# The last rows of a decoder layer: one PSUM bank of 512 columns against two of 256 columns with walked matmuls

## The chip, the cores and the metric

The kernel runs on one core of a Trainium2 chip. Its time is device time in microseconds, the median of several executions; a profile shows one of the executions instruction by instruction. The engines are TensorE (PE, with its weight loads as PEld), VectorE (DVE), ScalarE (ACT), GpSimd (POOL) and SyncE (SP), which issues most DMAs.

## What is computed

One decoder layer in fp32 for 256 prompt rows and 64 sample rows, 320 in all, with D = 2048 and D_FF = 5632. Cut to what matters here:

```
h = x + merged @ w_o
hn = rms_norm(h, g_ffn)
h = h + (silu(hn @ w_gate) * (hn @ w_up)) @ w_down
y = rms_norm(h, g_final)      # y * rsqrt(mean(y*y) + 1e-6) * g_final
```

The change lies in the product with w_down and in the final norm of the first 128 rows. That norm needs the squares of all 2048 columns of a row before it can scale any of them.

## The kernel before

**The precision.** Every fp32 matrix is split into a high part (rounded to the matmul's type, fp32r) and a low part (the rest). A product is made of high x high, high x low and low x high, so each weight tile is loaded raw by SP's queue, copied to `whi` by ACT and subtracted to `wlo` by DVE (`split_to`, L128). PE multiplies without a pause.

**The walk.** `turns` (L101) rearranges an access of s parts and j columns so that four columns of part 0 come first, then four of part 1, and so on. A matmul whose moving operand and output are both rearranged this way computes the same numbers in another order of columns. The rows in SBUF are laid out for it: their parts lie a multiple of 64 columns plus 16 apart (`rows_in`, L109; `a_rows`, L964), in the PSUM bank they lie exactly 64 apart (`fives` and `placed`, 5 parts and 8 parts).

**The down product.** `down(half, c0)` (L985) takes 512 output columns of w_down at a time, for 28 and then for 16 of the 44 blocks of D_FF. It makes the product in two forms at once. Four banks `dn` hold it by feature (features on partitions, rows as columns), with matmuls at L1008 (high weights) and L1016 (low weights), both walked. For the first 128 rows the low part of the activations is multiplied the other way round: the activations `a_low(k)` are the stationary operand and 512 columns of the high weights move, so that a bank holds rows on partitions and features as columns. That is the matmul of L1012, one per block k, not walked. For the first 1536 columns its bank is a `dl` from the pool aux2; for the last 512 (E0 = 1536 on) it is `rowacc`, which isn't read out after half 0 but kept.

**The tail.** For the last 512 columns of half 1 the order is written out by hand (from L1145). The weights of all 16 blocks are held in SBUF. The feature form comes first (L1173, L1178), and only for the 192 rows that need it. Then come 32 matmuls into `rowacc` (L1207), for each block one with `a_first(k)`, the high part of the first 128 rows, and one with `a_low(k)`. After the first 8 of them stand `pn` (L1211), the sum of squares over partitions for the other 192 rows, and four transposes (L1213) which add the first 128 rows of h from its feature form to `rowacc`.

Behind that run two strands. The other 192 rows: DVE makes their factor from pn, multiplies in five pieces (L1228), and SP sends each (L1229). The first 128 rows: ACT squares `rowacc` and sums over its columns (`row_squares`, L1084, the instruction at L1086, with a second one that reads the accumulator), DVE sums the earlier partial sums (L1232), ACT and DVE make the factor `rr` (L1235 to L1238), then DVE, ACT and POOL scale the columns of `y0` (L1240, L1241, L1245), DVE scales `rowacc` by rr and by gfb, the broadcast g_final (L1251), and five DMAs send `y0` (L1242).

`after(...)` fixes the order of issue without a wait on the chip.

Of the kernel before, what the change touches and what calls it, by code (L numbers as in the profile page):

```python
# [8 lines left out]
F32 = mybir.dt.float32  # L9
F32R = mybir.dt.float32r  # L10
AF = mybir.ActivationFunctionType
ALU = mybir.AluOpType
AX = mybir.AxisListType
PSUM = bass.MemoryType.PSUM

D = 2048
# [10 lines left out]
P = 128  # L27
KC = D // P
CW = 256
# [8 lines left out]
E0 = D - 512  # L38
# [14 lines left out]
def hybrid_layer(ctx: ExitStack, tc: tile.TileContext, a: dict, o: list):  # L53
    nc = tc.nc
# [11 lines left out]
    aux = [aux_p.enter_context(tc.tile_pool(name="aux", bufs=4, space=PSUM))]  # L66
# [5 lines left out]
    def ps_aux(name):  # L72
        return aux[0].tile([P, 512], F32, tag="aux", name=name)
# [3 lines left out]
    def u(s):  # L77
        uid[0] += 1
        return f"{s}_{uid[0]}"

    def after(*marks):

        es = ExitStack()
        for m in marks:
            es.enter_context(tc.issue_after(m.ins))
        return es
# [14 lines left out]
    def turns(ap):  # L101

        return ap.rearrange("p s (i b) -> p i s b", b=4)

    def fives(ap):

# [51 lines left out]
    last = {}  # L158
# [78 lines left out]
    ident = cst.tile([P, P], F32, name="ident")  # L237
# [37 lines left out]
    hT = xv[:, VW:VX].rearrange("p (k t) -> p k t", k=KC)  # L275
# [560 lines left out]
    for cp in range(4):  # L836
# [8 lines left out]
        for c in range(2):  # L845
# [13 lines left out]
            n = UL - 2  # L859
            nc.scalar.activation(cv[:, :n], ue[:, 0:n], AF.Copy, scale=wcv[:, ch:ch + 1])  # L860
            for jj in (1, 2):
                nc.vector.scalar_tensor_tensor(
                    cv[:, :n], ue[:, jj:jj + n], wcv[:, jj * 8 + ch:jj * 8 + ch + 1], cv[:, :n],
                    op0=ALU.mult, op1=ALU.add,
# [33 lines left out]
    for mp in range(8):  # L898
        c0 = mp * CW
# [51 lines left out]


    aux_p.close()
    aux[0] = ctx.enter_context(tc.tile_pool(name="aux2", bufs=3, space=PSUM))
    row_p = ctx.enter_context(tc.tile_pool(name="row_p", bufs=1, space=PSUM))
    rowacc = row_p.tile([P, 512], F32, name="rowacc")
    fp = ctx.enter_context(tc.tile_pool(name="fp", bufs=1))
    op = ctx.enter_context(tc.tile_pool(name="op", bufs=1))
    FH = (28, 16)
# [25 lines left out]
    def down(half, c0):  # L985

        nf, f0 = FH[half], half * FH[0]
        ps = [ps_acc(u("dn")) for _ in range(4)]
        low = ps_aux(u("dl")) if c0 < E0 else rowacc
        sets = [[k] for k in range(0, nf, 2)]  # L990
        sets[-2:] = [sets[-2] + sets[-1]]
        for i, k0s in enumerate(sets):
            parts = {}
            for k0 in k0s:
                raw = wp.tile([P, 2, 512], F32, tag="wraw", name=u("wraw"), bufs=4)
                nc.sync.dma_start(raw, w_d[c0 // 512, :, f0 + k0:f0 + k0 + 2, :])
                hi, lo = down_parts()
                split_to(hi, lo, raw)
                for j in range(2):
                    parts[k0 + j] = (hi[:, j, :], lo[:, j, :])  # L1000
            end = i == len(sets) - 1
            order = [(k, c) for k in parts for c in range(4)]
            if end or i == 0:
                order.sort(key=lambda kc: kc[1])
            for k, c, m in in_turn(order, 2 if end else 4):
                cs = slice(c * P, (c + 1) * P)
                if m == 0:
                    nc.tensor.matmul(  # L1008
                        turns(placed(ps[c])), parts[k][0][:, cs], turns(a_move(k)), start=k == 0, stop=False
                    )  # L1010
                elif m == 1 and c == (2 if k > k0s[0] + 1 else 0):
                    nc.tensor.matmul(  # L1012
                        low, a_low(k), parts[k][0], start=k == 0, stop=k == nf - 1 and c0 < E0
                    )
                elif m == 2:
                    last["mm"] = nc.tensor.matmul(  # L1016
                        turns(placed(ps[c])[:, :, 0:JT]), parts[k][1][:, cs], turns(a_move(k)[:, :, 0:JT]),
                        start=False, stop=k == nf - 1,
                    )
            if pending and (end or i == 3):  # L1020
                with after(last["lo"], last["hi"], last["mm"]):
                    pending.pop(0)()
        mark["out"] = []
        for c in range(4):
            k = c0 // P + c
            got, (first, rest) = placed(ps[c]), h_parts(k)
            nc.vector.tensor_add(first, first, got[:, :, 0:JR])
            nc.vector.tensor_add(rest, rest, got[:, :, JR:JT])
            mark["out"].append(nc.vector.tensor_add(rest, rest, got[:, :, JT:]))
        if c0 < E0:  # L1030
            ys = ylow[:, c0:c0 + 512].rearrange("p (a c f) -> p c a f", a=4, c=4)
            got = low.rearrange("p (c a f) -> p c a f", a=4, c=4)
            if half == 0:
                nc.scalar.activation(ys, got, AF.Copy)
            else:
                nc.vector.tensor_add(ys, got, ys)

    for half in range(2):
# [38 lines left out]
        if half == 1:  # L1077
            ya = xp.tile([P, 2, D], F32, tag="xh", name="ya")
            y0, gfb = ya[:, 0, :], ya[:, 1, :]
            nc.gpsimd.dma_start(gfb, a["g_final"].partition_broadcast(P))  # L1080
            ssf = op.tile([P, 5], F32, name="ssf")
            yacc = op.tile([P, TR], F32, name="yacc")

            def row_squares(i, src):  # L1084
                jk = op.tile([P, 512], F32, tag="jk", name=u("jk"))
                nc.scalar.activation(  # L1086
                    jk[:, :src.shape[-1]], src, AF.Square, scale=D ** -0.5, accum_out=ssf[:, i:i + 1]
                )

            turned = {}  # L1090

            def rows_turned(c0):

                x = op.tile([P, 512], F32, tag="jk", name=u("jk")).rearrange("p (b m) -> p b m", b=4)
                nc.vector.transpose(
                    x.rearrange("p b (c f) -> p c b f", c=4),
                    hT[:, c0 // P:c0 // P + 4, 0:P].rearrange("p c (b t) -> p c b t", b=4),
                )
                blocks_out([x[32 * b:32 * b + 32] for b in range(4)], x)
                turned[c0] = x.rearrange("p b m -> p (b m)")  # L1100

            def rows_of(c0):

                y = y0[:, c0:c0 + 512]
                nc.gpsimd.tensor_tensor(y, turned.pop(c0), ylow[:, c0:c0 + 512], op=ALU.add)
                row_squares(c0 // 512, y)
                nc.gpsimd.tensor_tensor(y, y, gfb[:, c0:c0 + 512], op=ALU.mult)

            def rest_square(k):
                sq = tmp("td", "sq")[:, :TR] if k else yacc  # L1110
                nc.scalar.activation(sq, hT[:, k, P:T], AF.Square)
                return sq

            def rest_factor(k):
                rest = hT[:, k, P:T]
                last["hi"] = nc.scalar.activation(rest, rest, AF.Copy, scale=g_fin[:, k:k + 1])

            def rest_of(chunks):

                for k in chunks:  # L1120
                    sq = rest_square(k)
                    if k:
                        nc.vector.tensor_add(yacc, yacc, sq)
                    rest_factor(k)

            warm = op.tile([P, 1], F32, name="warm")
            eps = op.tile([P, 1], F32, name="eps")
            nc.vector.memset(eps, EPS)
            nc.vector.memset(ssf[:, 3:4], EPS)
            with after(last["sig"]):  # L1130
                nc.scalar.activation(warm, ones, AF.Abs_reciprocal_sqrt)
# [8 lines left out]


    nf = FH[1]
    es = slice(E0, D)

    held = []  # L1145
    more = xp.tile([P, 5 * KT * CW + 64], F32R, tag="xl", name="more")
# [55 lines left out]
    for c in range(4):  # L1202
        rest_factor(E0 // P + c)

    for k in range(nf):
        for m, x in enumerate((a_first(k), a_low(k))):
            last["mm"] = nc.tensor.matmul(rowacc, x, held[k][0], start=False, stop=k == nf - 1 and m == 1)  # L1207
        if k == 3:
            with after(last["mm"]):
                pn = ps_aux("pn")  # L1210
                nc.tensor.matmul(pn[:, :TR], ones_r.bitcast(F32), yacc, start=True, stop=True)  # L1211
                for c in range(4):
                    last["mm"] = nc.tensor.matmul(  # L1213
                        rowacc[:, c * P:(c + 1) * P], hT[:, E0 // P + c, 0:P], ident, start=False, stop=False,
                        is_transpose=True,
                    )
    rf, v, t = (op.tile([P, TR], F32, name=n) for n in ("rf", "rv", "rt"))
# [7 lines left out]
    for k0, k1 in ((0, 2), (2, 5), (5, 10), (10, 15), (15, KC)):  # L1225
# [2 lines left out]
            ahead = (nc.vector.tensor_mul(yq, hT[:, k0:k1, P:T], rf.unsqueeze(1).to_broadcast([P, k1 - k0, TR])),)  # L1228
        nc.sync.dma_start(y_r[:, k0:k1, :], yq)  # L1229
    s3, v, r = (op.tile([P, 1], F32, name=n) for n in ("s3", "vf", "rr"))  # L1230
    with after(*ahead):
        nc.vector.tensor_reduce(s3, ssf[:, 0:4], axis=AX.X, op=ALU.add)  # L1232
    row_squares(4, rowacc)
    part = ssf[:, 4:5]
    nc.scalar.activation(r, part, AF.Abs_reciprocal_sqrt, bias=s3)  # L1235
    nc.vector.tensor_scalar(v, part, s3, -0.5, op0=ALU.add, op1=ALU.mult)
    nc.vector.scalar_tensor_tensor(v, r, r, v, op0=ALU.mult, op1=ALU.mult)
# [10 lines left out]
    send(768, 1280, nc.scalar)  # L1248
    with after(sent):
        sent = send(256, 768)  # L1250
    nc.vector.scalar_tensor_tensor(y0[:, es], rowacc, r, gfb[:, es], op0=ALU.mult, op1=ALU.mult)  # L1251
    with after(sent):
        sent = send(1280, E0)
    with after(sent):
# [80 lines left out]
```

## Time and profile before

| | us |
|---|---|
| median of 3 runs | 1592.32 (1591.9 to 1592.51) |
| the profiled execution | 1591.96 |
| its span, first to last instruction | 1590.3 |
| PE busy | 1582.1 |
| DVE busy | 889.6 |
| ACT busy | 645.7 |
| POOL busy | 133.1 |

The span is shorter than the execution's time by 1.66 us, which lie around it. A row of the page or of a view names an engine, a line of the kernel, the operation, what it writes and reads (out<-in), and durations. Durations of consecutive matmuls overlap; the chain of waits is the view that shows their pace. "128*128 128x256" is a matmul with 128 x 128 weights and 256 moving columns. The granted TensorE clock was 0.999 of full.

### The profile page before, as it was taken

The numbers are of one execution on the slowest core, as the hardware profiler recorded it, in microseconds if no ns is written. First come the engines' busy times: TensorE is split into PE (matmuls) and PEld (weight loads), VectorE is DVE, ScalarE is ACT, GpSimd is POOL, SyncE is SP. The second block draws the span as 40 slices with busy tenths as digits, with TensorE's granted clock in tenths as the row PEclk, the third lists the DMA queues.
The fourth block names the chain that finished last, engine by engine and source line by source line (L and its number), as shares of the span: only waits on it lengthen the run. The fifth ranks groups of instructions, "written<-read, shape, count | busy, mean of one in ns | idle before, by whom it ended". The sixth has DMA issues, their size and how long they took to land.

```text
span 1590.3 us, 26435 instructions
## 1 busy us (share of the span) xinstructions
PE 1582.1 (99%) x10890; PEld 1546.5 (97%) x10890; DVE 889.6 (56%) x1314; ACT 645.7 (41%) x917; POOL 133.1 (8%) x213
## 2 busy tenths in 40 slices
PE   9999999999999999999999999999999999999998
PEld 9999999999999999999999999998888999999887
DVE  7879765544455555555555555553444455555556
ACT  7554443333333334444333333333333334444443
POOL 1414331000000003320000000000000000000021
PEclk9999999999999999999999999999999999999999
DMA  7757566555454545554555544555555455545663
GB/s 272 207 182 224 171 211 208 159 159 158 153 156 157 159 159 157 154 155 158 159 158 154 157 156 159 159 159 160 157 154 157 156 159 159 156 155 155 190 188 125
DMA packets 77648, 266.06 MB, mean 167 GB/s; under 512 B 9832, under 2 KB 13112, under 8 KB 77400
## 3 DMA queue, kind: packets, MB, share of 16 engines
q1 hardware_dynamic: 71736, 249.99, 50.6%
q0 software_dynamic: 5360, 13.84, 3.0%
q8 instruction: 85, 1.39, 0.4%
q10 hardware_dynamic: 432, 0.56, 0.1%
q14 instruction: 35, 0.29, 0.1%
HBM read 257.27 MB, written 9.04 MB: 167 GB/s over the span
## 4 chain that ended last, share of the span: by engine, by line
PE 99%; DVE 0%; issue 0%; DVEq 0%; ACT 0%
PE fu L150 19%; PE fg L150 19%; PE dn L1008 9%; PE wo L150 7%; PE ga L150 7%; PE gc L150 7%; PE dn L1016 6%; PE B L150 3%; PE H L150 3%; PE C L150 3%; PE q L150 3%; PE ya L150 3%; PE yc L150 3%; PE dl L1012 2%; PE kv L150 2%; PE dn L1173 1%
## 5 line engine op out<-in xcount | busy, mean ns | idle before, releaser
L130 DVE TENSOR_TENSOR wlo<-wraw,whi 128x1024 fp32r<-128x1024 f32 (+1 forms) x460 | 562.8, 1225 | 562.9 <-ACT whi L129 451.6
L129 ACT ACTIVATE whi<-wraw 128x1024 fp32r<-128x1024 f32 (+1 forms) x460 | 485.5, 1056 | 721.1 <-PE fu L150 129.3
L150 PE MATMUL fu<-hh_t,whi 128*128 128x320 f32 x704 | 205.0, 301 | 0.0
L150 PE MATMUL fg<-hh_t,whi 128*128 128x320 f32 x704 | 205.0, 301 | 0.0
L150 PE MATMUL fu<-hl_t,whi 128*128 128x320 f32 x704 | 205.0, 301 | 0.0
L150 PE MATMUL fg<-hl_t,whi 128*128 128x320 f32 x704 | 205.0, 301 | 0.0
L150 PE MATMUL fu<-hh_t,wlo 128*128 128x320 f32 x704 | 158.8, 301 | 0.0
L150 PE MATMUL fg<-hh_t,wlo 128*128 128x320 f32 x704 | 158.8, 301 | 0.0
L1008 PE MATMUL dn<-a_t,whi 128*128 128x512 f32 x640 | 155.3, 382 | 0.0
L150 PEld LDWEIGHTS fu<-hh_t,whi 128*128 128x128 f32 x704 | 131.7, 187 | 0.0
L150 PEld LDWEIGHTS fu<-hl_t,whi 128*128 128x128 f32 x704 | 131.7, 187 | 0.0
L150 PEld LDWEIGHTS fg<-hl_t,whi 128*128 128x128 f32 x704 | 131.7, 187 | 0.0
L150 PEld LDWEIGHTS fg<-hh_t,whi 128*128 128x128 f32 x704 | 131.6, 187 | 0.0
L1008 PEld LDWEIGHTS dn<-a_t,whi 128*128 128x128 f32 x640 | 115.4, 187 | 16.5 <-issue 1.2
L150 PEld LDWEIGHTS fg<-hh_t,wlo 128*128 128x128 f32 x704 | 116.1, 187 | 0.0
L150 PEld LDWEIGHTS fu<-hh_t,wlo 128*128 128x128 f32 x704 | 116.1, 187 | 0.0
L1016 PEld LDWEIGHTS dn<-a_t,wlo 128*128 128x128 f32 x640 | 97.6, 188 | 6.9
L1016 PE MATMUL dn<-a_t,wlo 128*128 128x320 f32 x640 | 103.3, 301 | 0.0
L150 PE MATMUL gc<-xh_t,whi 128*128 128x320 f32 x256 | 74.5, 301 | 0.0
L150 PE MATMUL gc<-xl_t,whi 128*128 128x320 f32 x256 | 74.5, 301 | 0.0
L150 PE MATMUL ga<-xh_t,whi 128*128 128x320 f32 x256 | 74.5, 301 | 0.0
L150 PE MATMUL ga<-xl_t,whi 128*128 128x320 f32 x256 | 74.5, 301 | 0.0
(313 smaller groups left out, 2692.6 us busy)
## 6 DMA issues: line engine op xcount, KB each, us to landing
wraw<-in_w_in_dram SPq DMA_DIRECT2D x128, 512.0 KB, 3.9
wraw<-in_w_gate_dram SPq DMA_DIRECT2D x88, 512.0 KB, 3.8
wraw<-in_w_up_dram SPq DMA_DIRECT2D x88, 512.0 KB, 3.8
wraw<-in_w_down_dram SPq DMA_DIRECT2D x88, 512.0 KB, 3.7
wraw<-in_w_o_dram SPq DMA_DIRECT2D x32, 512.0 KB, 3.8
wraw<-in_w_conv_out_dram SPq DMA_DIRECT2D x16, 512.0 KB, 3.7
wraw<-in_w_attn_out_dram SPq DMA_DIRECT2D x16, 512.0 KB, 3.7
wraw<-in_w_kv_dram SPq DMA_DIRECT2D x6, 512.0 KB, 7.2
```

Source lines behind the costliest of these rows:

```text
L129: last["hi"] = nc.scalar.activation(hi, src, AF.Copy)
L130: last["lo"] = nc.vector.tensor_sub(lo, src, hi.bitcast(F32))
L150: last["mm"] = nc.tensor.matmul(way(fives(out)), w, way(x), **kw)
L1008: nc.tensor.matmul(turns(placed(ps[c])), parts[k][0][:, cs], turns(a_move(k)), start=k == 0, stop=False)
L1012: nc.tensor.matmul(low, a_low(k), parts[k][0], start=k == 0, stop=k == nf - 1 and c0 < E0)
L1016: last["mm"] = nc.tensor.matmul(turns(placed(ps[c])[:, :, 0:JT]), parts[k][1][:, cs], turns(a_move(k)[:, :, 0:JT]), start=False, stop=k == ...
L1173: nc.tensor.matmul(turns(placed(ps[c])[:, :, JR:]), held[k][0][:, cs], turns(a_move(k)[:, :, JR:]), start=k == 0, stop=k == nf - 1,)
```

## The change

The bank `rowacc` becomes two, `rowacc` for the columns E0 to E0 + 255 and `rowend` for the last 256, each a tile of a whole PSUM bank of which 256 columns are used. The pool aux2 gives up a buffer for it (3 become 2). Every matmul into them is split in two of 256 columns, and both its moving weights and its output are accessed as a walk of four parts of 64 columns. Unlike the rows' layout, the weights' four parts lie exactly 64 columns apart.

In the tail the loop over blocks runs twice, first for `rowacc`, then for `rowend`. `pn` and the transposes stand after 16 of the 64 matmuls, two of the transposes going to each bank. The first bank is squared on its own; DVE multiplies it by gfb into `y0` before the sums are reduced; the reduce takes five partial sums instead of four. When rr is there, only the second bank is scaled out of PSUM, and the first 256 columns are scaled within SBUF like the other columns.

```diff
+    def quarters(ap):
+
+        return turns(ap.rearrange("p (s j) -> p s j", s=4))
...
-    aux[0] = ctx.enter_context(tc.tile_pool(name="aux2", bufs=3, space=PSUM))
+    aux[0] = ctx.enter_context(tc.tile_pool(name="aux2", bufs=2, space=PSUM))
...
-    rowacc = row_p.tile([P, 512], F32, name="rowacc")
+    rowacc = [row_p.tile([P, 512], F32, name=n)[:, :CW] for n in ("rowacc", "rowend")]
...
-        low = ps_aux(u("dl")) if c0 < E0 else rowacc
+        low = ps_aux(u("dl")) if c0 < E0 else None
+        lows = [low] if c0 < E0 else rowacc
...
-                    nc.tensor.matmul(
-                        low, a_low(k), parts[k][0], start=k == 0, stop=k == nf - 1 and c0 < E0
-                    )
+                    for h, d in enumerate(lows):
+                        n = 512 // len(lows)
+                        w = parts[k][0][:, h * n:h * n + n]
+                        nc.tensor.matmul(
+                            d if low is not None else quarters(d), a_low(k),
+                            w if low is not None else quarters(w), start=k == 0,
+                            stop=k == nf - 1 and c0 < E0,
+                        )
...
-    for k in range(nf):
+    for h, k in ((h, k) for h in range(2) for k in range(nf)):
         for m, x in enumerate((a_first(k), a_low(k))):
-            last["mm"] = nc.tensor.matmul(rowacc, x, held[k][0], start=False, stop=k == nf - 1 and m == 1)
-        if k == 3:
+            last["mm"] = nc.tensor.matmul(
+                quarters(rowacc[h]), x, quarters(held[k][0][:, h * CW:h * CW + CW]), start=False, stop=k == nf - 1 and m == 1
+            )
+        if h == 0 and k == 7:
...
-                        rowacc[:, c * P:(c + 1) * P], hT[:, E0 // P + c, 0:P], ident, start=False, stop=False,
+                        rowacc[c // 2][:, c % 2 * P:c % 2 * P + P], hT[:, E0 // P + c, 0:P], ident, start=False, stop=False,
...
+    row_squares(4, rowacc[0])
     with after(*ahead):
-        nc.vector.tensor_reduce(s3, ssf[:, 0:4], axis=AX.X, op=ALU.add)
-    row_squares(4, rowacc)
-    part = ssf[:, 4:5]
+        ahead = (nc.vector.tensor_mul(y0[:, E0:E0 + CW], rowacc[0], gfb[:, E0:E0 + CW]),)
+    with after(*ahead):
+        nc.vector.tensor_reduce(s3, ssf[:, 0:5], axis=AX.X, op=ALU.add)
+    row_squares(5, rowacc[1])
+    part = ssf[:, 5:6]
...
-    nc.vector.scalar_tensor_tensor(y0[:, es], rowacc, r, gfb[:, es], op0=ALU.mult, op1=ALU.mult)
+    nc.vector.scalar_tensor_tensor(
+        y0[:, E0 + CW:], rowacc[1], r, gfb[:, E0 + CW:], op0=ALU.mult, op1=ALU.mult
+    )
+    mul(E0, E0 + CW)
```

How the instructions stand in a row shows it at three places. The first is PE in half 0, within one set of two blocks of the last 512 columns; `whi` are the high weights, `a_t` the activations, and the numbers behind the names are the program's own. Before:

```order
L1008 MATMUL dn_12345<-a_t_7540,whi_12349 128x16x8x4 x2
L1012 MATMUL rowacc<-whi_12349,a_t_7540 128x512 x2
L1016 MATMUL dn_12343<-a_t_7540,wlo_12350 128x10x8x4 x2
L1016 MATMUL dn_12344<-a_t_7540,wlo_12350 128x10x8x4 x2
L1016 MATMUL dn_12345<-a_t_7540,wlo_12350 128x10x8x4 x2
```

And in the same place now, with the lines of the changed kernel:

```order
L1013 MATMUL dn_12346<-a_t_7541,whi_12350 128x16x8x4 x2
L1020 MATMUL rowacc<-whi_12350,a_t_7541 128x16x4x4
L1020 MATMUL rowend<-whi_12350,a_t_7541 128x16x4x4
L1020 MATMUL rowacc<-whi_12350,a_t_7541 128x16x4x4
L1020 MATMUL rowend<-whi_12350,a_t_7541 128x16x4x4
L1026 MATMUL dn_12344<-a_t_7541,wlo_12351 128x10x8x4 x2
```

Two matmuls of 512 columns in a row have become four walked ones of 16 x 4 x 4 columns, which go to the two banks in turn; nothing else has moved there. The second place is PE at the program's end, where `a_t` and `more` also hold some of the weights. Before:

```order
L1207 MATMUL rowacc<-a_t_12695 128x512 x8
L1211 MATMUL pn<-yacc,ones_r 128x192
L1213 MATMUL rowacc<-ident,xv 128x128 x4
L1207 MATMUL rowacc<-a_t_12695 128x512 x4
L1207 MATMUL rowacc<-more,a_t_12695 128x512 x8
```

And now:

```order
L1216 MATMUL rowacc<-a_t_12724 128x16x4x4 x12
L1216 MATMUL rowacc<-more,a_t_12724 128x16x4x4 x4
L1222 MATMUL pn<-yacc,ones_r 128x192
L1224 MATMUL rowacc<-ident,xv 128x128 x2
L1224 MATMUL rowend<-ident,xv 128x128 x2
L1216 MATMUL rowacc<-more,a_t_12724 128x16x4x4 x4
L1216 MATMUL rowacc<-whi_15593,a_t_12724 128x16x4x4 x4
L1216 MATMUL rowacc<-whi_15599,a_t_12724 128x16x4x4 x4
L1216 MATMUL rowacc<-whi_15605,a_t_12724 128x16x4x4 x4
L1216 MATMUL rowend<-a_t_12724 128x16x4x4 x12
```

All 32 of `rowacc` now stand ahead of the 32 that fill `rowend`, and pn stands behind as many columns as before. The third place is DVE at the end, behind its last multiply for the other 192 rows. Before:

```order
L1228 TENSOR_TENSOR wraw_15809<-xv,rf 128x192
L1232 TENSOR_REDUCE s_15820<-ssf 128x1
L1236 TENSOR_SCALAR vf<-ssf,s_15820 128x1
L1237 SCALAR_TENSOR_TENSOR vf<-rr,vf 128x1
L1238 SCALAR_TENSOR_TENSOR rr<-vf,rr 128x1
L1240 TENSOR_SCALAR ya<-ya,rr 128x256
L1240 TENSOR_SCALAR ya<-ya,rr 128x512
L1251 SCALAR_TENSOR_TENSOR ya<-rowacc,rr,ya 128x512
```

And now:

```order
L1239 TENSOR_TENSOR wraw_15870<-xv,rf 128x192
L1244 TENSOR_TENSOR ya<-rowacc,ya 128x256
L1246 TENSOR_REDUCE s_15881<-ssf 128x1
L1250 TENSOR_SCALAR vf<-ssf,s_15881 128x1
L1251 SCALAR_TENSOR_TENSOR vf<-rr,vf 128x1
L1252 SCALAR_TENSOR_TENSOR rr<-vf,rr 128x1
L1254 TENSOR_SCALAR ya<-ya,rr 128x256
L1254 TENSOR_SCALAR ya<-ya,rr 128x512
L1265 SCALAR_TENSOR_TENSOR ya<-rowend,rr,ya 128x256
L1254 TENSOR_SCALAR ya<-ya,rr 128x256
```

The multiply by gfb stands between the five multiplies and the reduce, and the one of 512 columns at the end has become two of 256. On ACT the square of 512 columns has become one of `rowacc` and one of `rowend`, with nothing between them. The rows of SP and POOL are the same.

More of the change, by code (lines that the diff above doesn't have):

```diff
@@ L1080, in hybrid_layer @@
             nc.gpsimd.dma_start(gfb, a["g_final"].partition_broadcast(P))
-            ssf = op.tile([P, 5], F32, name="ssf")
+            ssf = op.tile([P, 6], F32, name="ssf")
             yacc = op.tile([P, TR], F32, name="yacc")
@@ L1142, in hybrid_layer @@
     nf = FH[1]
-    es = slice(E0, D)
     held = []
```

## The prediction

> **What bounds the kernel now.** I read the page first, then the chain of waits of the last 16 us, then the engines' busy time over the last microseconds.
>
> ```profile
> span 1590.3 us, 26435 instructions
> PE 1582.1 (99%) x10890; PEld 1546.5 (97%) x10890; DVE 889.6 (56%) x1314; ACT 645.7 (41%) x917; POOL 133.1 (8%) x213
> PE 99%; DVE 0%; issue 0%; DVEq 0%; ACT 0%
> ```
>
> TensorE (PE) is busy from end to end, and the chain that ended last runs through it for 99% of the span. So a nanosecond saved on a matmul anywhere moves the end by as much, and so does one saved behind the last matmul. The chain of waits, each row a start, a length and what ran:
>
> ```profile
> 1576.58 0.37 PE pn L1211 x2
> 1576.95 0.44 PE rowacc L1213 x4
> 1577.39 5.54 PE rowacc L1207 x24
> 1582.97 0.47 issue
> 1583.44 0.20 ACT jk L1086
> 1583.67 0.30 ACT rr L1235
> 1584.00 0.23 DVE vf L1237
> 1584.25 0.17 DVE rr L1238
> 1584.45 0.35 DVE ya L1240
> 1584.80 0.62 DVEq L1323
> 1585.42 0.66 DVE ya L1251
> ```
>
> The last 24 matmuls into the one bank end at about 1582.95. Then ScalarE (ACT) squares 512 columns and reads its accumulator (0.47 + 0.20), VectorE (DVE) and ACT make the factor rr (0.30 + 0.23 + 0.17), and the rows are scaled and sent. What follows is a matter of transfers; the busy time by stretches shows it (length, then PE, PEld, DVE, ACT, POOL, granted clock, share of the DMA engines, GB/s):
>
> ```profile
> 1582.00:1584.00 2.00, 0.91 (x4) 0.39 (x3) 0.60 (x4) 0.98 (x3) 0.00 (x0) 1.00 1.01 405
> 1584.00:1586.00 2.00, 0.00 (x0) 0.00 (x0) 1.93 (x5) 0.72 (x1) 1.06 (x1) 1.00 0.42 150
> 1586.00:1588.00 2.00, 0.00 (x0) 0.00 (x0) 0.08 (x1) 0.00 (x0) 0.00 (x0) 0.55 1.02 384
> ```
>
> Over 1586 to 1588 the DMA engines are full with the 1 MB of y0, over 1584 to 1586 they are idle for 58%. So the end of the span is the moment at which rr is ready, plus one fixed run of transfers: what makes rr earlier moves the end one for one, what makes the last DVE multiply a little later hides behind the queue. There is room for that shift: the transfers of the other rows leave about 1.2 us idle before those of y0.
>
> **Part 1: the matmuls of half 0.** The columns from E0 on accumulate 28 matmuls here. The chain in that stage, and the group:
>
> ```profile
> 1218.22 1.12 PE dn L1016 x8
> 1219.34 1.76 PE dn L1008 x8
> 1221.10 0.46 PE rowacc L1012 x2
> L1012 PE MATMUL rowacc<-whi,a_t x28: 389/390/390, 1213.8 to 1257.9; 128*128 128x512 f32 x28
> ```
>
> The durations of 390 ns overlap; the pace from start to start is what the chain shows. Contiguous 512 columns: 0.46 / 2 = 230 ns. Walked matmuls of the same type: 512 columns 1.76 / 8 = 220 ns, 320 columns 1.12 / 8 = 140 ns. Between these two a column costs 80 / 192 = 0.417 ns, and 320 columns are 133 of their 140. A walked matmul thus costs 0.417 ns a column and some 7 ns, and one of 256 columns 140 - 64 x 0.417 = 113.3 ns. The third walked shape, and the first matmuls of the tail, from the same chain later on:
>
> ```profile
> 1567.22 1.34 PE dn L1173 x8
> 1573.46 0.70 PE dn L1173 x4
> 1574.73 1.85 PE rowacc L1207 x8
> ```
>
> 384 columns at 1.34 / 8 = 167.5 ns lie on the line (166.7), but the four at 0.70 / 4 = 175 ns, which all go to one bank, do not: up to 7.5 ns more, as the tail's matmuls will all go to one bank too.
>
> No row has 256 walked columns. The nearest are 256 contiguous columns, each matmul with a weight load of its own as here:
>
> ```profile
> 90.31 0.23 PE ps L573 x2
> 90.66 0.23 PE ps L573 x2
> L573 PEld LDWEIGHTS ps<-k,at_t x32: 187/188/189, 90.0 to 169.1; 128*128 128x128 f32 x32
> L573 PE MATMUL ps<-k,at_t x32: 278/280/281, 90.1 to 169.2; 128*128 128x256 f32 x32
> ```
>
> They go at 115 ns, so halving the columns and doubling the loads costs next to nothing even without a walk, and the four transposes of L1213, 128 columns each, at 0.44 / 4 = 110 ns bound the pace of a weight load from above. I take 113.3; the ends are 110 (paced by the load) and 121 (113.3 and the 7.5 of one bank). Half 0: 14 pairs x 0.46 = 6.44 us become 56 x 0.1133 = 6.35 us: **-0.09** (-0.28 to +0.34).
>
> [...]
>
> **Part 2: the matmuls of the tail.** 32 become 64, in two rounds of 32, the first bank's first. The first 8 (1.85 us) become 16 (1.81 us) ahead of pn, but that 0.04 is lost, since pn's weight load already stands waiting for yacc (first row; then four more rows of the same view for the parts below):
>
> ```profile
> 1576.36 0.30 PEld L1211 LDWEIGHTS pn<-yacc,ones_r 128*128 128x128 f32 x2 [0.21 <-DVE yacc L1198]
> 1578.69 3.63 DVE L1228 TENSOR_TENSOR wraw<-xv,rf 128x384 f32<-128x384 f32 x5
> 1582.24 0.15 DVE L1232 TENSOR_REDUCE s<-ssf 128x1 f32<-128x4 f32 x1
> 1582.95 0.60 ACT L1086 ACTIVATE jk<-rowacc 128x512 f32<-128x512 f32 x1 [5.23 <-PE rowacc L1207]
> 1585.34 0.74 DVE L1251 SCALAR_TENSOR_TENSOR ya<-rowacc,rr,ya 128x512 f32<-128x512 f32 x1
> ```
>
> The other 24 (5.54 us) become 48 x 0.1133 = 5.44 us: **-0.10** (-0.26 to +0.27 by the same ends). The transposes stay four of 128 columns.
>
> **Part 3: the square.** The first bank is full after 32 of the 64, about 3.6 us before the end; ACT has been idle for 5.23 us there, so that square (and its read of the accumulator) costs nothing. Behind the last matmul stands a square of 256 columns in place of 512. The slope of ACT by size:
>
> ```profile
> L1086 ACT ACTIVATE jk<-ya 128x512 f32<-128x512 f32 x1 | 0.6, 632 | 1.4 <-POOL ya L1105 1.4
> L1111 ACT ACTIVATE sq<-xv 128x192 f32<-128x192 f32 x4 | 1.5, 366 | 2.9 <-DVE xv L1191 2.9
> L601 ACT ACTIVATE s<-s,mx x32: 386/388/403, 96.3 to 175.5; 128x128 f32<-128x128 f32 x32
> ```
>
> Squares: (632 - 366) / 320 = 0.83 ns a column; against the exponentials of L601, (632 - 388) / 384 = 0.64. For 256 columns **-0.21** (at the other end -0.16).
>
> **Part 4: what DVE gets.** Ahead of the reduce stands a new multiply of the first bank by gfb, 256 columns from PSUM. The nearest rows, and that of a multiply within SBUF:
>
> ```profile
> L584 DVE TENSOR_TENSOR s<-ps,bias x8: 406/410/416, 92.7 to 171.9; 128x256 f32<-128x256 f32 x8
> L815 DVE SCALAR_TENSOR_TENSOR qt<-q,rb x8: 412/424/425, 48.6 to 87.1; 128x256 f32<-128x256 f32 x8
> L1240 DVE TENSOR_SCALAR ya<-ya,rr 128x256 f32<-128x256 f32 x1 | 0.4, 352 | 0.0
> ```
>
> Behind the five multiplies of L1228, which end at 1582.32, the reduce ends at about 1582.39 + 0.41 = 1582.80. It is first needed with the accumulator, now at 1583.67 and then at about 1583.36: 0.56 us of cover, and nobody else waits for DVE there. **0**; if that multiply took the 0.74 of L1251, still 0. It also moves behind the same five multiplies, so the sends of the other rows on SP's queue keep their places. At the end the one multiply of 512 columns from PSUM (0.74) becomes one of 256 from PSUM (0.42) and one of 256 in SBUF (0.35): 0.77 less some 0.08 of overlap (L1251 is 0.74 long by its row and 0.66 by the chain). **0**, and the full DMA queue hides 0.1 either way. The pool aux2 has 2 buffers instead of 3; each dl is read out at the end of its own call of down(), a call before its buffer comes round again, and pn comes last of all: **0**.
>
> **The sum.** -0.09 - 0.10 - 0.21 = -0.40 us. The profiled execution took 1591.96 us, 1590.3 of it span; the median of the three runs is 1592.32 (1591.9 to 1592.51), so 0.36 above. From the median: 1591.9 us. All costs at one end give -0.28 - 0.26 - 0.21 = -0.75, at the other +0.34 + 0.27 - 0.16 = +0.45. A measurement of this kernel tells some 0.2%, 3.2 us, from no change; the forecast is far inside.
>
> **Rivals.**
>
> *The new pace eats the gain (0.17).* 256 columns at 121 ns or more: then the 56 and the 48 cost 104 x 7.7 ns = 0.8 us above 113.3 each, twice what the change saves, and the time is 1591.92 + 0.80 = 1592.7; at 130 ns it is 1593.7. For it: the 175 ns rows. Against: 115 ns of L573, whose consecutive pairs go to one bank too.
>
> *The walk through the weights is slow (0.04), the slower side.* Every walked operand of before reads rows whose parts lie a multiple of 64 columns plus 16 apart; the new walk reads a weight row in parts exactly 64 apart, and no row shows such a read. If pieces of parts so placed hinder one another, the stream could fall to that of pn, which is the slowest here, 192 columns in 0.37 / 2 = 185 ns, 0.96 ns a column: 247 ns for 256 columns, and 104 x 0.134 = +13.9 us over the forecast, 1605.8. It decides from about 148 ns on: 3.2 us and the 0.40 saved elsewhere, over 104 matmuls, are 35 ns each. For it: the padding itself. Against: the bank's own parts lie exactly 64 apart in the walked rows of before, and they are the faster ones.
>
> *The added loads show (0.01).* 60 more weight loads of up to 110 ns each, not hidden, would be +6.6 us, 1598.5. Against: 140 ns for 320 columns leave 7 ns for everything but the stream, and L573 has a load of its own within its 115. [...]
>
> *The change doesn't do what it says (within the first rival).* Were the first square held back behind the second bank, both would stand in the chain: the 0.21 goes, and at most one more read of the accumulator (0.20) comes, so 1592.32 - 0.19 = 1592.1 to 1592.3. The order of ACT puts the two squares one behind the other with nothing between, so nothing holds the first.
>
> **Chances.** Forecast 0.77, pace 0.17, walk 0.04, loads 0.01, and 0.01 for a gain over 3.2 us that I can't derive (the tail's matmuls and the half's are 13.8 us in all). Faster 0.01, same 0.94, slower 0.05. Range: the ends from the median, 1591.6 and 1592.8, widened below by the 0.4 that separates the median from the fastest run, and above to the low part of the first rival: 1591.2 to 1592.9.
>
> **What would show it.** Right: the four new matmuls of a set in half 0 at 0.45 us together, where two stood at 0.46; the last 48 of the tail at 5.3 to 5.6 us; an ACT row of 256 columns of about 0.38 us behind the last matmul; the reduce done before the second accumulator is read. Wrong: matmul starts over 121 ns apart, a weight load that ends an idle stretch of PE, a DVE row between the accumulator and rr, or DMA engines idle between 1586 and 1588.

## The result: 2.7 us slower, and the profile after

| | before | changed |
|---|---|---|
| median of 21 runs each, us | 1592.12 (1591.44 to 1592.81) | 1594.83 (1593.93 to 1595.37) |
| ratio to before | | 1.0017 (95%: 1.0011 to 1.0023) |
| the profiled execution, us | 1591.96 | 1595.03 |
| its span, us | 1590.3 | 1593.3 |

Two of the executions counted further down ran at a far lower granted clock (one of before at 0.654, 2312.52 us, and one of the kernel over padded rows at 0.85, 1780.94 us), and the ratios leave them out. The forecast was 1591.9, in a range up to 1592.9; the time lies 1.9 us above the range. The page of the changed kernel, its span and the sums by engine:

```profile
span 1593.3 us, 26560 instructions
PE 1585.3 (99%) x10950; PEld 1552.2 (97%) x10950; DVE 891.4 (56%) x1316; ACT 646.0 (41%) x919; POOL 133.5 (8%) x213
```

TensorE still bounds the kernel for 99%, and it is busy 3.2 us longer. No engine has taken its place, so the loss must lie in the matmuls themselves. The chain of waits in half 0, two sets one after the other (start, length, what ran):

```profile
1218.21 0.14 PE rowacc L1020
1218.35 0.13 PE rowend L1020
1218.48 0.14 PE rowacc L1020
1218.62 0.14 PE rowend L1020
1218.76 1.13 PE dn L1026 x8
1219.89 1.76 PE dn L1013 x8
...
1222.20 1.14 PE dn L1026 x8
```

Four matmuls take 0.55 us where two took 0.46 and the forecast had 0.45. Over the 56 of the stage it is 136.4 ns each from start to start, not 113.3, and over the 121 that the prediction named as the first sign of being wrong. The eight matmuls of 320 columns behind them take 1.13 to 1.14 instead of 1.12, too. The chain at the tail:

```profile
1576.74 2.16 PE rowacc L1216 x16
1578.90 0.33 PE pn L1222 x2
1579.23 0.22 PE rowacc L1224 x2
1579.44 0.22 PE rowend L1224 x2
1579.66 2.17 PE rowacc L1216 x16
1581.83 4.31 PE rowend L1216 x32
1586.14 0.02 issue
1586.16 0.02 ACTq L1096
1586.18 0.04 issue
1586.22 0.07 ACT jk L1096
1586.29 0.21 issue
1586.51 0.20 ACT jk L1096
...
1586.73 0.30 ACT rr L1249
```

The last 48 take 2.17 + 4.31 = 6.48 us, 135 ns each, where 24 took 5.54 and the forecast had 5.44. The first 16 take 2.16 where eight took 1.85. What stands behind the last matmul went nearly as forecast. The instructions of the square's line on ACT, then those of DVE around the reduce:

```profile
L1096 ACT ACTIVATE jk<-rowacc x1: 403/403/403, 1581.9 to 1581.9; 128x256 f32<-128x256 f32 x1
L1096 ACT ACTIVATE jk<-rowend x1: 384/384/384, 1586.2 to 1586.2; 128x256 f32<-128x256 f32 x1
```

```profile
1580.98 3.64 DVE L1239 TENSOR_TENSOR wraw<-xv,rf 128x384 f32<-128x384 f32 x5
1584.53 0.42 DVE L1244 TENSOR_TENSOR ya<-rowacc,ya 128x256 f32<-128x256 f32 x1
1584.87 0.15 DVE L1246 TENSOR_REDUCE s<-ssf 128x1 f32<-128x5 f32 x1
1586.73 0.21 DVE L1250 TENSOR_SCALAR vf<-ssf,s 128x1 f32<-128x1 f32 x1 [1.72 <-ACT jk L1096]
1588.40 0.47 DVE L1265 SCALAR_TENSOR_TENSOR ya<-rowend,rr,ya 128x256 f32<-128x256 f32 x1
```

The first square runs at 1581.9, 4.3 us before the last matmul ends, and costs nothing. The second is read out 0.29 us after its start (1586.22 to 1586.51, the chain), where the square of 512 took 0.49 (1582.95 to 1583.44). The second square also starts 0.08 us behind the last matmul (1586.14 to 1586.22), before 0.02 (1582.93 to 1582.95): ACT's queue now has an instruction of its own ahead of it, the row ACTq, which the forecast did not count. The reduce is done at 1585.02, 1.7 us before it is needed. From the end of the last matmul to the end of the span it is 7.19 us, before 7.34.

So the time went to three places. Summed from start to start over half 0's stage in the two traces, its low matmuls take 7.64 us in place of 6.38 (+1.26) and the dn matmuls between them 38.37 in place of 37.93 (+0.44). The tail, from its first low matmul to its last, takes 9.41 in place of 8.20 (+1.21, the six rows above against the four of before). Behind it, -0.15. Together +2.76, against +2.71 of the medians. (The changed kernel's execution also reached half 0 some 0.27 us later, in a part in which the two kernels do the same. The executions below scatter there by more, and mostly stages are compared from here on.)

### The profile page after: what moved, and what is told of

It reads as the page before. It is cut to its first block, busy times and chain, and to the rows that moved or that the text cites. A ratio compares the mean times of both kernels' runs of the same rounds, so it can differ in the third digit from the quotient of the medians.

```text
span 1593.3 us, 26560 instructions
## 1 busy us (share of the span) xinstructions
PE 1585.3 (99%) x10950; PEld 1552.2 (97%) x10950; DVE 891.4 (56%) x1316; ACT 646.0 (41%) x919; POOL 133.5 (8%) x213
## 4 chain that ended last, share of the span: by engine, by line
PE 99%; DVE 0%; DVEq 0%; ACT 0%; issue 0%; ACTq 0%
PE fu L154 19%; PE fg L154 19%; PE dn L1013 9%; PE wo L154 7%; PE ga L154 7%; PE gc L154 7%; PE dn L1026 6%; PE B L154 3%; PE H L154 3%; PE C L154 3%; PE q L154 3%; PE ya L154 3%; PE yc L154 3%; PE dl L1020 2%; PE kv L154 2%; PE dn L1182 1%
## 5 line engine op out<-in xcount | busy, mean ns | idle before, releaser
L1013 PEld LDWEIGHTS dn<-a_t,whi 128*128 128x128 f32 x640 | 115.4, 187 | 16.5 <-issue 1.2
```

The lines of the kernel that those rows point to most:

```text
L1013: nc.tensor.matmul(turns(placed(ps[c])), parts[k][0][:, cs], turns(a_move(k)), start=k == 0, stop=False)
```

## The experiments

Three theories were to be told apart: **the read** (the weight rows are read in parts exactly 64 columns apart, which the prediction named as a rival), **the write** (the walked bank), and **the loads** (twice as many weight loads). All could make 135 ns out of 113.

**No walk at all.** Two banks, contiguous:

```
     def quarters(ap):
-        return turns(ap.rearrange("p (s j) -> p s j", s=4))
+        return ap
```

> Two banks of 256 columns as in the changed kernel, but their 120 matmuls read and write their columns contiguously. Three theories for the 135 ns that the walked matmuls took from start to start where 113 were forecast. Read: the walk through the weights, in parts exactly 64 columns apart, slows the moving operand. Load: a weight load needs some 135 ns, and 256 columns no longer hide it. Write: the walk through the bank slows the output. Read and write expect 115 to 118 ns here and a time of about 1592.9 us, 104 x 18 ns less than the changed kernel's 1594.83; load expects 135 ns still and 1594.8.

```profile
1574.80 1.90 PE rowacc L1216 x16
...
1577.46 1.89 PE rowacc L1216 x16
1579.35 3.80 PE rowend L1216 x32
```

These rows of its chain give 118 to 119 ns each; half 0's go at 116. The median is 1592.26 (11 runs; before 1591.87 in 21), ratio 1.0002 (0.9993 to 1.0011). The loads are as many as in the changed kernel, so they are not the cause. It is the walk, and two contiguous banks gain nothing. The 1592.9 expected counted 104 matmuls alone; with the walk went also 0.36 us of the dn matmuls in half 0 and 0.26 of the tail's first 16.

**Half of the walk each.** First only the bank is walked, then only the weights; the columns of the first 128 rows land at other places in both, so their last 512 are not the product:

```
-    quarters(rowacc[h]), x, quarters(held[k][0][:, h * CW:h * CW + CW])
+    quarters(rowacc[h]), x, straight(held[k][0][:, h * CW:h * CW + CW])
```

```
-    quarters(rowacc[h]), x, quarters(held[k][0][:, h * CW:h * CW + CW])
+    straight(rowacc[h]), x, quarters(held[k][0][:, h * CW:h * CW + CW])
```

(`straight` keeps the three dimensions of the access and reads in order; half 0 likewise.)

> As the changed kernel, but only the output is walked; the weights are read contiguously, so that columns land at other places than they should. Write and load expect 135 ns from start to start, read expects 113 to 118.

> As the changed kernel, but only the weights are walked; the output is contiguous, so that columns land at other places than they should. Read and load expect 135 ns from start to start, write expects 113 to 118.

The chain with the bank walked alone, then with the weights walked alone:

```profile
1575.17 1.90 PE rowacc L1221 x16
...
1577.83 1.89 PE rowacc L1221 x16
1579.72 3.80 PE rowend L1221 x32
```

```profile
1576.77 2.16 PE rowacc L1221 x16
...
1579.69 2.17 PE rowacc L1221 x16
1581.86 4.31 PE rowend L1221 x32
```

To the digit the first is the kernel without a walk (1592.44 us) and the second is the changed kernel (1595.16; one execution each). The whole loss is in reading the weights; how the bank is written makes no difference here: 118 to 119 ns with and without that walk.

**The same walk over padded rows.** Both walked, but the weights' place is taken by the activations' rows, whose parts stand a multiple of 64 plus 16 apart (the last 512 columns of the first 128 rows are not the product):

```
-    quarters(rowacc[h]), x, quarters(held[k][0][:, h * CW:h * CW + CW])
+    quarters(rowacc[h]), x, turns(a_move(k)[:, 4 * h:4 * h + 4, :])
```

> As the changed kernel, output and moving operand walked in four parts, but the moving columns are taken from the activations' padded rows, whose parts lie a multiple of 64 columns plus 16 apart, instead of the weights; the last 512 columns of the first 128 rows are thus not the product. Read, if it is the spacing of exactly 64 that hurts, expects 113 ns and about 1592.5 us; load and write expect 135 ns and about 1594.8.

```profile
1575.75 1.84 PE rowacc L1216 x16
...
1578.40 1.84 PE rowacc L1216 x16
1580.24 3.69 PE rowend L1216 x32
```

115 ns in the tail and 113.2 in half 0, the forecast's pace: 1592.46 (10 runs), ratio 1.0002 (0.9992 to 1.0012). It isn't lower than before. In the profiled execution its low matmuls took a little less than those of before (0.05 us in half 0), but the dn matmuls of 512 columns in half 0 took 0.5 us more together (225.5 ns each where they take 220.4). Why was not found.

This run changed the tile along with the distance. The next takes the distance alone.

**Other distances in the same weight rows.** Four parts of 64 columns, at 68 (the tail's first bank), 80 (its second), 72 and 96 (half 0):

```
+    def spaced(row, h, by):
+        o = h * (512 - 4 * by)
+        return turns(row[:, o:o + 4 * by].rearrange("p (s j) -> p s j", s=4)[:, :, 0:64])
...
-    quarters(rowacc[h]), x, quarters(held[k][0][:, h * CW:h * CW + CW])
+    quarters(rowacc[h]), x, spaced(held[k][0], h, (68, 80)[h])
```

> The changed kernel, with the four parts of 64 columns of the same weight rows at another distance, so that the last 512 columns of the first 128 rows are not the product: 68 apart in the tail's first bank, 80 in its second, 72 and 96 in half 0's two. Theory (parts that stand a multiple of 64 apart hinder one another, whatever tile they lie in): at 80 (64 and 16, as in the rows of the activations) 113 to 115 ns, 3.6 to 3.7 us for 32; at 96, 72 and 68 under 125 ns too, nearer to 135 the smaller the step beyond 64 if what collides is a stretch of several pieces; the time 1592.0 to 1593. Rival (the weights' tiles are slow to walk because of where they lie or who writes them, not the distance; the padded run read another tile): 135 ns at all four distances, 1595.

```profile
1575.47 1.93 PE rowacc L1221 x16
...
1578.16 1.93 PE rowacc L1221 x16
1580.09 3.71 PE rowend L1221 x32
```

121 ns at 68 and 116 at 80; in half 0 116 at 72 and 120 at 96; the time 1592.78 (one execution). The tile is not the cause: four columns of distance more take two thirds of the loss away, 16 more all but 1 ns of it. That the pace would be the nearer to 135 the smaller the step beyond 64 is not borne out.

**Other numbers of parts, and the whole product again.** In the first kernel the tail's banks are read as 2 parts of 128 and 8 of 32, half 0 as 16 of 16; in the second as 16 of 16 and 32 of 8, half 0 as 32 of 8:

```
-    def quarters(ap):
-        return turns(ap.rearrange("p (s j) -> p s j", s=4))
+    def quarters(ap, s=4, b=4):
+        return ap.rearrange("p (s i b) -> p i s b", s=s, b=b)
...
+    quarters(rowacc[h], *((2, 4), (8, 4))[h]), x, quarters(held[k][0][:, h * CW:h * CW + CW], *((2, 4), (8, 4))[h])
```

> The product as in the changed kernel, with the same pieces of four columns, but other numbers of parts: the tail's first bank is walked as 2 parts of 128, its second as 8 parts of 32, half 0 as 16 parts of 16 (weights and bank alike). Theory (pieces that follow one another a multiple of 64 columns apart hinder one another): the first 32 of the tail go at 135 ns (2.16 us for 16, as with 4 parts), the last 32 at 113 to 118 ns (3.6 to 3.8 us), half 0 at 113 to 118 ns; the time about 1592.7 (before, and the one slow round of the tail: 32 x 20 ns = 0.65 us). Rival one (every walk through unpadded weights is slow): 135 ns or more in all three places, 1595. Rival two (every distance that is a power of two is slow, the smaller the worse): 135 ns for the 2 parts, more than that for 8 and for 16.

> As the kernel with 2 and 8 parts, but 16 parts of 16 columns in the tail's first bank, 32 parts of 8 in its second and in half 0. Theory of the multiple of 64: 113 to 118 ns in all three places (tail 1.8 to 1.9, 1.8 to 1.9 and 3.6 to 3.8 us), 1592.0 to 1592.3. Rival one (every walk through unpadded weights): 135 ns everywhere, 1595. Rival two (powers of two): above 135 ns everywhere, over 1595.

The tail of the one and of the other:

```profile
1577.92 1.98 PE rowacc L1216 x16
1579.90 3.92 PE rowend L1216 x32
```

```profile
1577.36 1.92 PE rowacc L1216 x16
1579.28 3.78 PE rowend L1216 x32
```

2 parts (128 apart): 124 to 127 ns; 8 (32 apart): 122.5; 16 (16 apart): 117 to 120 in the tail and 113 in half 0; 32 (8 apart): 118. The times are 1592.72 and 1591.96 (one execution each). Both rivals fall, for the walk through unpadded weights can go at 113, and 8 and 16 parts are faster than 4, not slower. But my theory was too simple as well. It had 135 for 2 parts and 113 to 118 for 8. A reading that fits the 2 parts is that only every other step goes from one part to the next, 128 on; the others go back. It was not tested by itself, and the 122.5 of the 8 parts stays without an account.

**Larger pieces.** Four parts of 64, 8 columns from each at a time in the tail's first bank and 16 in its second (32 in half 0):

```
+    quarters(rowacc[h], *((4, 8), (4, 16))[h]), x, quarters(held[k][0][:, h * CW:h * CW + CW], *((4, 8), (4, 16))[h])
```

> Four parts of 64 as in the changed kernel, but larger pieces: 8 columns from a part at a time in the tail's first bank, 16 in its second, 32 in half 0. If each change of part costs (64 changes a matmul cost the 20 ns, 0.3 ns each), the pace falls from 135 ns to about 125 (16 in 2.0 us), 120 (32 in 3.84 us) and, in half 0, 117. Rival (four parts exactly 64 apart collide however long the piece): 135 ns in all three places, 1595. Rival (pieces of 16 bytes alone are slow): 115 to 119 ns in all three, 1592.2.

```profile
1578.19 2.03 PE rowacc L1216 x16
1580.22 3.75 PE rowend L1216 x32
```

127 ns with pieces of 8, 117 with 16, 118.5 in half 0 with 32. So the cost falls with the number of steps from one part to the next, as the first of the three theories had it (125, 120 and 117).

**One bank of 512, walked.** The kernel before with 8 parts of 64 (half 0 likewise):

```
-    last["mm"] = nc.tensor.matmul(rowacc, x, held[k][0], ...)
+    last["mm"] = nc.tensor.matmul(eighths(rowacc), x, eighths(held[k][0]), ...)
```

> The kernel before, with its one bank of 512 columns and its 60 low matmuls, walked as 8 parts of 64, weights and bank. If the cost of the distance goes by the column (135 - 113 = 22 ns for 256), a matmul of 512 takes 220 + 44 = 264 ns: half 0's pairs 0.53 in place of 0.46, the tail's 24 some 6.3 us in place of 5.54, the time 1591.9 + 60 x 33 ns = 1593.9. Rival (it goes by the matmul, as a wait at its start or for its weights): 242 ns, 5.8 us for 24, 1592.6. Rival (8 parts behave otherwise than 4): under 230 ns, 1591.9 or less.

```profile
1576.19 2.21 PE rowacc L1211 x8
...
1579.16 6.64 PE rowacc L1211 x24
```

277 ns in place of 231: +46 for 512 columns, where 256 cost some 17 over their contiguous 118.5. So it is no wait once for each matmul, for which 242 ns were expected; by the column 264 were. It goes roughly by the step: of a walk by fours, 48 steps of 64 in 256 columns cost 135 - 118.5 = 16.5 ns (0.34 each), 112 in 512 cost 46 (0.41), and 32 steps of 128 some 6 to 8 (about 0.2), all against a contiguous read. Against the walk over padded rows, 115 ns, the 48 cost 20 (0.42 each), so the price of a step is known only to within that. The time was 1594.88 (one execution).

**The change with 16 parts.** One number is another, the product is whole:

```
-        return turns(ap.rearrange("p (s j) -> p s j", s=4))
+        return turns(ap.rearrange("p (s j) -> p s j", s=16))
```

> The changed kernel with one number changed: the walk takes 16 parts of 16 columns in place of 4 of 64, everywhere; the product as before. Theory (the distance of exactly 64 is the whole loss): half 0 at 113 ns as in the run with 16 parts there (its stage 44.1 us, as before), the tail at 117 ns (8.45 us against 8.34), 0.14 less behind the last matmul; together within 0.2 us of the kernel before, 1591.8 to 1592.3, and 2.5 us under the changed kernel. Rival (two banks and twice the matmuls cost by themselves, whatever the walk): 1593 or more.

```profile
1574.93 1.87 PE rowacc L1216 x16
1576.80 0.35 PE pn L1222 x2
...
1577.58 1.81 PE rowacc L1216 x16
1579.39 3.64 PE rowend L1216 x32
```

The last 48 take 5.45 us (113.5 each; the forecast for the change was 5.44), half 0's go at 113.1. Median 1591.92 (11 runs; before 1592.03 in 21), ratio 0.9999 (0.9990 to 1.0008). The loss of 2.7 us is gone with one number of the walk. By stages, half 0 takes 0.09 less than before, the tail 0.09 and the end 0.13: 0.3 us, of which the times can't tell anything. The forecast's sum was 0.40: with this walk its mechanism holds.

The same round of 16 matmuls in the same walk took 1.92 us in the kernel with 16 and 32 parts and takes 1.81 here, 120 and 113 ns. So differences of 7 ns between the walks above say little of the distance; the 135 lies 15 over the highest of these.

**All low matmuls walked, one bank; then the tail's alone.** The experiments pointed to a gain for 512 columns, too, in parts of 16 (the dl of the other columns included; half 0's last columns in parts of 8):

```
+    cut(low, 32 if c0 < E0 else 64), a_low(k), cut(parts[k][0], 32 if c0 < E0 else 64), ...
...
+    last["mm"] = nc.tensor.matmul(cut(rowacc, 32), x, cut(held[k][0], 32), ...)
```

> The kernel before, its one bank kept, with all low matmuls of 512 columns walked: those of dl (132) and the tail's 32 as 32 parts of 16, half 0's 28 as 64 parts of 8. If the 16 parts that went at 113 ns for 256 columns show the stream without hindrance, 512 columns take 220 to 222 ns in place of 228 to 230: 192 x 7 ns = 1.3 us less, 1590.6. Rival (each change of part costs its 0.1 ns also here, 128 changes): 230 ns and over, 1592 or more.

> The kernel before with its one bank, the tail's 32 matmuls of 512 columns walked as 32 parts of 16, half 0 and dl contiguous. By the stage of the run that walked all of them, 8.17 in place of 8.34 us for the tail: 0.17 us less, 1591.8 where before is 1591.9, a difference that the times cannot show and the trace must: 24 in 5.37 us. Rival (the gain there came with the walk of the matmuls ahead): 5.5 us for the 24 and the time of before.

The last 24 in the first, with one pair of its dl and the dn matmuls behind it (1.12 us in the kernel before), and the last 24 in the second:

```profile
1541.88 0.46 PE dl L1016 x2
1542.34 1.14 PE dn L1020 x8
...
1579.51 5.37 PE rowacc L1211 x24
```

```profile
1577.44 5.60 PE rowacc L1211 x24
```

Neither holds. With all walked it took 1593.96 (one execution) where 1590.6 was expected. Its dl matmuls went from 228 to 230 ns (+0.30 us over the 132) and half 0's from 228 to 231. Most of the loss is not in the walked matmuls: the 640 of dn with 320 columns, which were not touched, went from 140.1 to 142.7 ns, +1.69 us by their starts. The tail alone gave 1591.96 (11 runs), ratio 0.9999 (0.9990 to 1.0008), with 233 ns for the same matmuls that took 224 in the kernel with all walked. So the pace of one and the same walk can differ by some 10 ns in 512 columns; what sets it was not found, and no version here beats the kernel before by what can be measured.

## Why the prediction was wrong

**Parts 1 and 2 failed, at one step: "I take 113.3; the ends are 110 (paced by the load) and 121".** The forecast for the low matmuls was -0.09 - 0.10; they gave +1.70 (1.26 of their own, 0.44 of the dn matmuls between them) and +1.21. The line from 320 to 512 columns was drawn through walks whose parts stand a multiple of 64 plus 16 apart, and applied to one at 64. The line itself is good: 113 to 115 ns over padded rows, 113.1 to 113.5 in the change with 16 parts. So the size was right for a walk that the kernel did not make. The weight loads did not show, as forecast (113 ns with a load for each).

**The rival "The walk through the weights is slow" had the cause** and 0.04. Two things were wrong with it. Its one argument against, that the bank's own parts stand exactly 64 apart and are fast, speaks of a write, and the runs with one side walked show that here the write said nothing of the read: 118 to 119 ns with the bank walked alone, 135 with the weights walked alone. And its price was taken from the slowest row at hand, pn's, at 247 ns, with 148 ns as the point from which it decides. It came to 135 to 136, below that point, and so the time is slower by less than the 0.2% that the prediction took for the least it could tell, yet far outside the range. An end of the range belonged to it: no row of before bounded that read, and 121 was the end of another case.

**The rival "The new pace eats the gain"** had the range of paces and not the cause. At 136.4 and 135 ns its sum gives 56 x 23.1 + 48 x 21.7 = 2.3 us over the forecast, 1594.2. It started from 1592.32, the median of three runs, 0.20 over the 1592.12 of the 21 here, so 0.8 us are missing to the 1594.8. They are the 0.06 that part 3 fell short, the 0.44 of the dn matmuls around the slow ones, which neither rival priced, and the first 16 of the tail: with pn they take 2.16 + 0.33 = 2.49 in place of 1.85 + 0.37 = 2.22, where the forecast put nothing because they would end sooner than pn's load is ready. They end later, and each ns of that counts, 0.27 us in all.

**Part 3** (-0.21): right in kind. The accumulator is read 0.20 us earlier after the start of the square; the square starts 0.06 later, behind the instruction on ACT's queue, and 0.15 reached the end of the span. **Part 4** (0): right; the new multiply took 0.42, as L584's row had it, and there was 1.7 us of cover instead of 0.56, since the last bank came later. "The added loads show" falls with the contiguous kernel, and "The change doesn't do what it says" with the first square's place.

What stays open is the mechanism: by the estimates above a step between parts 64 or 128 columns apart costs some 0.2 to 0.4 ns, and one between parts 80 apart next to nothing (116 ns a matmul, against 115 over padded rows); why, no run shows. Open is also why the dn matmuls next to the low ones change their pace: by +0.44 us here, but by +0.64 over padded rows, where the low matmuls were fast.

## What to carry to other kernels

Before an access pattern gets a price from others of its shape, compare the distance of its pieces with theirs, for the read and for the write apart. Here a distance of 64 columns in place of 80 made a matmul longer by a sixth (135 against 116 ns). Where no row shows an access, its price belongs into the range, however the other rows stand, and a kernel of one edited line (no walk, or another number of parts) prices it. And price and read a whole stage, not only the instructions that were edited: matmuls that nobody touched added a third in half 0 (0.44 to 1.26 us), and nearly the whole loss in the kernel with all low matmuls walked (1.69 us).

## What the runs showed of the hardware

Pace of a matmul of 256 columns of 4 bytes (fp32r) with its own weight load, by the walk through its moving operand in SBUF (pieces of 4 columns if not said otherwise; tail, from the chains):

| parts and distance in columns | ns |
|---|---|
| contiguous | 118 to 119 |
| 4 x 64, 64 apart | 135 |
| the same, pieces of 8 / 16 | 127 to 128 / 117 |
| 4 x 64, 68 apart / 80 apart | 121 / 116 |
| 4 x 64, rows padded to 64 n + 16 | 115 |
| 2 x 128, 128 apart | 124 to 127 |
| 8 x 32 / 16 x 16 / 32 x 8 | 122.5 / 113 to 120 / 118 |

The range at 16 x 16 is that of one walk in several programs, and each of the other rows is from one or two, so rows 7 ns apart or less are not ranked by this.

A piece of four columns is 16 bytes long in all the walks by fours alike, and still their pace differs by up to 22 ns (113 with 16 x 16, 135 with 4 x 64).

Walking the bank in PSUM, on the other hand, cost nothing at the distance of 64 (118 to 119 ns either way), and a weight load for every 256 columns none that shows, down to 113 ns.
